# Gate and up by seven products: the first weight tile of a pair is split earlier, and its differences move on GpSimd

## The chip, the cores and the metric

The kernel runs on one core of a Trainium2 chip. Five engines work beside each other, each through its own instructions in program order: TensorE (PE, matmuls), VectorE (DVE), ScalarE (ACT), GpSimd (POOL) and SyncE (SP), whose queue issues the DMAs. The time is the device time of one execution in microseconds, the median of several runs. Lower is better.

## The reference

The program computes four transformer layers over 512 tokens of width 1024 in float32: two hybrid layers (retention, dilated attention, spatial gating) and two of a second kind (sparse attention or convolution, then cross attention). Each ends in the same feed-forward block, which is all that the change touches:

```python
def swiglu(xn, w_gate, w_up, w_down):
    return (jax.nn.silu(xn @ w_gate) * (xn @ w_up)) @ w_down
```

The hidden width is 2816, 22 column blocks of 128.

## The kernel before

**Float32 from three products.** Each operand is split into a high half (rounded to fp32r) and a low half (the rest), and `mm3` (lines 384 to 387) adds up high x high, high x low and low x high. For a weight tile of 128 x 1024 the high half is a cast on ScalarE and the low half a subtraction on VectorE. Line 249 and 250 do this for plain tiles in `pump`, line 266 and 270 for the tiles of a pair.

**Gate and up.** `ffn` (line 565) runs four times, once a layer. Column blocks 0 and 1 are computed plainly at the start, beside the end of the work before. Blocks 2 to 21 go two by two, once for gate and once for up, by seven products in the place of eight (Strassen's scheme in Winograd's form): 10 block pairs, two each, so 20 **units** a stage. A unit takes a pair of weight tiles: a first tile `a` with the blocks b11 and b21, a second tile `b` with b12 and b22. `W.unit()` (line 257) prepares them in place by named steps:

- `cast1`, `low1`: the first tile's high half (ScalarE L266) and low half (VectorE L270)
- `t13`: two differences of 128 x 512 on GpSimd (L283 and L284), which overwrite the first tile's b11 and the second tile's b12, and so come after cast1 and low1
- `cast4`, `low4`: the halves of b22 as it was (512 wide)
- `t24`: two more differences on VectorE (L287 and L288), which read what L283 wrote
- `cast2`, `low2`: the halves of the second tile, which is now t3 and t2
- `cast3`, `low3`: the halves of the first tile, which is now t1 and t4

`seven(i)` (line 668) issues the seven products of unit i, 12 matmuls of 128 x 256 each: a11 and a12 with slot s1, then s4, twice s2, twice s3. Behind each product a step `s0` to `s6` reads PSUM and prepares the units that follow: m1 is copied on ScalarE (L700), VectorE adds (L705, L714, L718, L723, L724), and at `s0` of the next unit `whole_sum` (L684), for a gate unit with a Silu on ScalarE (L686), or, for an up unit, a product of gate and up (L690).

**What sets the order.** The program order of the code is each engine's order; nothing is reordered by a planner here. Before the change, during unit i, cast1 of unit i+2 stands at s6, low1 of unit i+1 at s0, t13 at s1, t24 and cast2 at s4, low2 and cast3 at s5, low3 at s6. So low1 and the two GpSimd differences come in the first quarter of a unit and are wanted by t24 in its middle. Weight tiles come by DMA on SP's queue, the first tiles into three buffers, the second into two; a buffer is freed at low3 and low2. A split takes one of eight `hl` slots in turn.

**PSUM.** The third product lies in bank 2 in even units and in bank 7 in odd ones (line 672).

**Around the stage.** At its start `transposer` (line 399) turns the normalized input; behind its casts (L395) copies of the last two token blocks (L417) go to a buffer from which the sums of the scheme are made (`whole`, L629, two of them on GpSimd; `mix`, L633). During the last unit `W.pump(1)` after each product begins to split the down product's weight tiles, and `hsplit` (line 744) splits the hidden blocks: block 0 after the sixth product, block 1 behind the stage. The down product (line 788) then takes all eight banks, two for each of four token blocks.

Of the kernel before, what the change touches and what calls it, by code (L numbers as in the profile page):

```python
# [199 lines left out]
class _Weights:  # L200
# [53 lines left out]
            if not moved:  # L254
                return

    def unit(self):

        V, S, G = self.nc.vector, self.nc.scalar, self.nc.gpsimd
        u = {}  # L260

        def cast(name, src, n=D):
            def go():
                if name not in u:
                    u[name] = self.slot()
                S.copy(u[name][:, 0, :n], src())  # L266
            return go

        def low(name, src, n=D):
            return lambda: V.tensor_sub(u[name][:, 1, :n], src(), u[name][:, 0, :n].bitcast(F32))  # L270

        def fetch():
            while self.widths[self.split] > 0:
                self.pump(1, True)
            self.prefetch()
            u["a"], u["j"] = self.r.pop(self.split), self.split + 1
            self.split += 2
            u["b11"], u["b21"] = (u["a"][:, 512 * i:512 * i + 512] for i in range(2))

        def t13():  # L280
            b = u["b"] = self.r.pop(u["j"])
            u["b12"], u["b22"] = (b[:, 512 * i:512 * i + 512] for i in range(2))
            G.tensor_sub(u["b11"], u["b12"], u["b11"])  # L283
            G.tensor_sub(u["b12"], u["b12"], u["b22"])  # L284

        def t24():
            V.tensor_sub(u["b22"], u["b22"], u["b11"])  # L287
            V.tensor_sub(u["b21"], u["b21"], u["b22"])  # L288

        def free(i):  # L290
            def go():
                self.held[i] -= 1
                self.prefetch()
            return go
        one, two, last = (lambda: u["a"]), (lambda: u["b"]), (lambda: u["b22"])
        u["do"] = {
            "cast1": (fetch, cast("s1", one)), "low1": (low("s1", one),), "t13": (t13,), "t24": (t24,),
            "cast2": (cast("s2", two),), "low2": (low("s2", two), free(1)), "cast4": (cast("s4", last, 512),),
            "low4": (low("s4", last, 512),), "cast3": (cast("s3", one),), "low3": (low("s3", one), free(0)),
        }  # L300
        for k, slot, i in (("b11", "s1", 0), ("b21", "s1", 1), ("t3", "s2", 0), ("t2", "s2", 1), ("b22", "s4", 0),
                           ("t1", "s3", 0), ("t4", "s3", 1)):
            u["w" + k] = lambda slot=slot, i=i: [
                u[slot][:, z, 512 * i:512 * i + 512].rearrange("p (a c) -> p a c", c=P) for z in range(2)]
        return u
# [17 lines left out]
def tile_mixers(ctx: ExitStack, tc: tile.TileContext, a: dict, widths: list, out: bass.AP):  # L323
# [48 lines left out]
    def bank(i):  # L372
        return psum.tile([P, T], F32, tag=f"b{i}", name=f"b{i}")
# [25 lines left out]
    def transposer(xn, t, dst, banks):  # L399
        dh, dl = dst  # L400

        def go(halves=(0, 1)):
            for half in halves:
                b = bank(banks[half])
                for kk in range(4):
                    k = 4 * half + kk
                    PE.transpose(b[:, kk * P:(kk + 1) * P], xn[:, k * P:(k + 1) * P], ident)  # L407
                ks = slice(4 * half, 4 * half + 4)
                if dl is None:
                    S.copy(dh[:, ks, cols(t)], blocks(b))  # L410
                else:
                    split_from(dh[:, ks, cols(t)], dl[:, ks, cols(t)], blocks(b))
                    if keep["x"] is not None and dh is xh and t > 1:
                        kept.append((keep["x"][half][:, :, (t - 2) * P:(t - 1) * P], blocks(b)))
                        keep["t"].add(t)
            while kept:
                S.copy(*kept.pop(0))  # L417
        return go

    turned = {}  # L420
# [144 lines left out]
    def ffn(pend, post, nxt, last=False):  # L565
# [82 lines left out]

        def unit(i):
            if i not in ops:  # L650
                ops[i] = W.unit()
            return ops[i]

        def prep(i, *names):
            if 0 <= i < len(units):
                for name in names:
                    for f in unit(i)["do"][name]:
                        f()
# [9 lines left out]
        def seven(i):  # L668


            n, j = units[i]
            b1, b2, b3, b6, b7, b45 = (bank(k) for k in (0, 1, 2 + 5 * (i % 2), 3, 4, 5 + i % 2))
            p1, p2, p3, p6, p7 = (z[:, :256] for z in (b1, b2, b3, b6, b7))
            p4, p5 = b45[:, :256], b45[:, 256:]
            m1, u2, u3, u4 = (st["pc"][:, 256 * k:256 * k + 256] for k in range(4))
            if not j:
                c = hraw[:, n:n + 2, :]
            elif n + 2 < NF:
                c = hraw[:, n + 2:n + 4, :]
            else:  # L680
                c = base.tile([P, D], F32, tag="xn", name="up", bufs=2).rearrange("p (a c) -> p a c", a=2)

            def whole_sum():
                V.tensor_add(c[:, :, 256:], u3[:, None, :].to_broadcast([P, 2, 256]), halves(b45))  # L684
                if not j:
                    S.activation(c, c, AF.Silu)  # L686

            def gated():
                if j:
                    V.tensor_mul(hraw[:, n:n + 2, :], hraw[:, n:n + 2, :], c)  # L690
            done.append((whole_sum, gated))
            last = done[-2] if i else (lambda: None,) * 2

            def s0():
                last[0]()
                W.done(int(i > 0))
                prep(i + 1, "low1")

            def s1():
                S.copy(m1, p1)  # L700
                prep(i + 1, "t13")
                last[1]()

            def s2():
                V.tensor_add(c[:, 0, TOK[0]], m1, p2)  # L705
                prep(i + 1, "cast4")
                W.done()

            def s3():
                prep(i + 1, "low4")  # L710
                W.done()

            def s4():
                V.tensor_add(u2, m1, p6)  # L714
                prep(i + 1, "t24", "cast2")

            def s5():
                V.tensor_add(u3, u2, p7)  # L718
                prep(i + 1, "low2", "cast3")
                W.done()  # L720

            def s6():
                V.tensor_add(u4, u2, p5)  # L723
                V.tensor_add(c[:, 1, TOK[0]], u4, p3)  # L724
                prep(i + 1, "low3")
                prep(i + 2, "cast1")
            todo = (("a11", "b11", p1), ("a12", "b21", p2), ("s4", "b22", p3), ("s2", "t2", p6), ("s3", "t3", p7), ("s1", "t1", p5),
                    ("a22", "t4", p4))
            for r, (p, f) in enumerate(zip(todo, (s0, s1, s2, s3, s4, s5, s6))):
                product(i, *p)  # L730
                f()
                if i == 0 and r == 0:
                    sum_low("s1", 3)()
                if i == len(units) - 1:
                    if r == 5:
                        hsplit(0)
                    W.pump(1)
                W.prefetch()
                yield

# [3 lines left out]
        def hsplit(k):  # L744
            if k < NF and k not in hsp:
                t = shared()
                split_from(t[:, 0:T], t[:, T:2 * T], hraw[:, k, :])
                hsp[k] = (t[:, 0:T], t[:, T:2 * T])

        def also(i, *fs):  # L750
            us, g = steps[i]
            steps[i] = (us, lambda: (g(), [f() for f in fs]))
        late = len(steps) - 4
        keep.update(x=(quarter(full(0)), quarter(full(3))), t=set())

        def fill(t):
            if t not in keep["t"] and turned[t]:
                for half in range(2):
                    z = [y[:, 4 * half:4 * half + 4, cols(t)].bitcast(F32) for y in (xh, xl)]
                    G.tensor_add(keep["x"][half][:, :, (t - 2) * P:(t - 1) * P], *z)  # L760
                keep["t"].add(t)

        def unit0(*names):
            return lambda: prep(0, *names)
        also(0, whole(1, 0, 0, G), unit0("cast1"))
        also(1, whole(2, 4, 0, G), unit0("low1"))
        also(2, lambda: fill(2))
        also(late - 1, lambda: fill(2), lambda: fill(3), lambda: keep.update(x=None), unit0("t13", "cast4"), mix(3, 0, 3, 1), mix(4, 3, 1, 0), mix(2, 2, 4, 0),
             sum_high("s2", 4), sum_high("s4", 2))
        also(late, unit0("low4"), sum_low("s4", 2), unit0("t24", "cast2"), sum_low("s2", 4))  # L770
        also(late + 1, unit0("low2"), mix(0, 0, 1, 0), sum_high("s3", 0))
# [8 lines left out]
            g = seven(i)  # L780
            steps += [(12 * 0.119, lambda g=g: next(g))] * 7
        steps.append((0, last_sums))
        steps.append((0, lambda: (two(0), nxt(), hsplit(1))))

        TAIL = 4
        acc = {}
# [1197 lines left out]
```

## Time and profile before

| what | us |
|---|---|
| median of 3 runs (2798.55 to 2804.01) | 2798.68 |
| the profiled execution | 2799.59 |
| its span, first to last instruction | 2797.8 |
| TensorE busy | 2677.8 (96%) |
| VectorE busy | 1809.4 (65%) |
| ScalarE busy | 1182.2 (42%) |
| GpSimd busy | 782.4 (28%) |

The profile covers one execution. A row of the timeline gives start, duration, engine, line, operation, out<-in, size and count; in brackets the idle time before it and what ended it. `raw` is a weight tile as loaded, `hl` its split, `sh` a split activation or hidden block, `xh` and `xl` the split input, `pc` the buffer of m1, u2, u3 and u4, `hraw` the hidden values, `b` a PSUM bank. Busy TensorE includes the time in which matmuls overlap, so its share says little of how close to its pace it is. The four stages start at about 281, 894, 1700 and 2448 us.

### The profile page before, as it was taken

The numbers are of one execution on the slowest core, as the hardware profiler recorded it, in microseconds if no ns is written. First come the engines' busy times: TensorE is split into PE (matmuls) and PEld (weight loads), VectorE is DVE, ScalarE is ACT, GpSimd is POOL, SyncE is SP. The second block draws the span as 40 slices with busy tenths as digits, with TensorE's granted clock in tenths as the row PEclk, the third lists the DMA queues.
The fourth block names the chain that finished last, engine by engine and source line by source line (L and its number), as shares of the span: only waits on it lengthen the run. The fifth ranks groups of instructions, "written<-read, shape, count | busy, mean of one in ns | idle before, by whom it ended". The sixth has DMA issues, their size and how long they took to land.

```text
span 2797.8 us, 41468 instructions
## 1 busy us (share of the span) xinstructions
PE 2677.8 (96%) x16568; PEld 2378.7 (85%) x16568; DVE 1809.4 (65%) x2733; ACT 1182.2 (42%) x2015; POOL 782.4 (28%) x662
## 2 busy tenths in 40 slices
PE   8999999999999999999999999999998889999999
PEld 7888999889788999878677889998886578899987
DVE  4555888545565888453985437887379744488852
ACT  3434444333434444333444434444256544344431
POOL 3231333002232232012451312331049913133300
PEclk9999999999999999999999999999999999999999
DMA  4221232323121323423232212333232312133331
GB/s 154 78 68 67 91 106 98 130 75 108 61 80 53 102 98 101 138 70 102 64 124 83 91 38 91 106 103 124 91 119 91 113 30 92 46 91 106 99 116 65
DMA packets 76225, 256.42 MB, mean 92 GB/s; under 512 B 10368, under 2 KB 11776, under 8 KB 76032
## 3 DMA queue, kind: packets, MB, share of 16 engines
q1 hardware_dynamic: 76032, 253.77, 28.3%
q8 instruction: 130, 2.13, 0.3%
q14 instruction: 63, 0.52, 0.1%
HBM read 251.64 MB, written 2.10 MB: 91 GB/s over the span
## 4 chain that ended last, share of the span: by engine, by line
PE 51%; DVE 23%; POOL 12%; ACT 10%; issue 4%; DMA 1%; POOLq 0%; ACTq 0%; DVEq 0%; SPq 0%
PE b L385 15%; PE b L387 15%; PE b L386 14%; DVE hl L270 8%; ACT hl L266 5%; POOL raw L283 5%; POOL raw L284 4%; DVE raw L287 2%; DVE hl L250 2%; DVE b L1759 2%; DVE hraw L684 2%; ACT hl L249 1%; PE b L407 1%; PE b L1639 1%; DVE xn L430 1%
## 5 line engine op out<-in xcount | busy, mean ns | idle before, releaser
L385 PE MATMUL b<-xh,hl 128*128 128x256 f32 (+1 forms) x1728 | 505.5, 293 | 4.0 <-DVE xn L457 2.4
L386 PE MATMUL b<-xl,hl 128*128 128x256 f32 (+1 forms) x1728 | 504.1, 292 | 1.7 <-DVE xl L396 1.7
L387 PE MATMUL b<-xh,hl 128*128 128x256 f32 (+1 forms) x1728 | 503.6, 291 | 0.0
L266 ACT CAST hl<-raw 128x1024 fp32r<-128x1024 f32 x320 | 286.7, 941 | 391.1 <-DVE raw L287 391.1
L385 PE MATMUL b<-hl,xh 128*128 128x512 f32 (+2 forms) x1152 | 439.1, 381 | 4.9 <-ACT xh L395 3.1
L386 PE MATMUL b<-hl,xh 128*128 128x512 f32 (+2 forms) x1152 | 422.6, 367 | 1.7 <-DVE hl L250 1.7
L387 PE MATMUL b<-hl,xl 128*128 128x512 f32 (+2 forms) x1152 | 423.0, 367 | 0.2
L270 DVE TENSOR_TENSOR hl<-raw,hl 128x1024 fp32r<-128x1024 f32 x320 | 387.1, 1210 | 9.4 <-ACT hl L266 1.3
L250 DVE TENSOR_TENSOR hl<-raw,hl 128x1024 fp32r<-128x1024 f32 (+2 forms) x249 | 303.4, 1232 | 137.8 <-ACT hl L249 135.7
L249 ACT CAST hl<-raw 128x1024 fp32r<-128x1024 f32 (+2 forms) x308 | 303.5, 1000 | 101.9 <-PE b L387 60.1
L385 PEld LDWEIGHTS b<-xh,hl 128*128 128x128 f32 x1728 | 331.4, 192 | 11.4 <-issue 3.4
L386 PEld LDWEIGHTS b<-xl,hl 128*128 128x128 f32 x1728 | 331.3, 192 | 7.8 <-DVE xl L396 2.7
L387 PEld LDWEIGHTS b<-xh,hl 128*128 128x128 f32 x1728 | 331.2, 192 | 5.4
L283 POOL TENSOR_TENSOR raw<-raw 128x512 f32<-128x512 f32 x80 | 140.2, 1752 | 567.3 <-DVE hl L270 502.7
L387 PE MATMUL b<-hl,sh 128*128 128x512 f32 x704 | 276.3, 392 | 7.2 <-DVE sh L396 7.2
L385 PE MATMUL b<-hl,sh 128*128 128x512 f32 x704 | 276.7, 393 | 2.2 <-ACT sh L395 2.2
L387 PE MATMUL b<-sh,hl 128*128 128x256 f32 x960 | 270.8, 282 | 5.8 <-DVE hl L270 5.8
L386 PE MATMUL b<-hl,sh 128*128 128x512 f32 x704 | 276.0, 392 | 0.0
L385 PE MATMUL b<-sh,hl 128*128 128x256 f32 x960 | 269.2, 280 | 1.1 <-ACT hraw L576 1.1
L386 PE MATMUL b<-sh,hl 128*128 128x256 f32 x960 | 267.9, 279 | 0.0
L385 PEld LDWEIGHTS b<-hl,xh 128*128 128x128 f32 x1152 | 219.3, 190 | 35.1 <-issue 7.0
L386 PEld LDWEIGHTS b<-hl,xh 128*128 128x128 f32 x1152 | 219.4, 190 | 25.9 <-DVE hl L250 3.0
(304 smaller groups left out, 4745.2 us busy)
## 6 DMA issues: line engine op xcount, KB each, us to landing
raw<-in_ws SPq DMA_DIRECT2D x400, 512.0 KB, 3.6
raw<-in_ws SPq DMA_DIRECT2D x64, 384.0 KB, 3.1
x<-in_x SPq DMA_DIRECT2D x4, 512.0 KB, 6.6
mem<-in_mem SPq DMA_DIRECT2D x4, 512.0 KB, 5.6
out<-x SPq DMA_DIRECT2D x4, 512.0 KB, 2.6
raw<-in_ws SPq DMA_DIRECT2D x4, 336.0 KB, 2.8
gain<-in_g_mix_pre SPq DMA_DIRECT2D x2, 512.0 KB, 4.7
gain<-in_g_mix_post SPq DMA_DIRECT2D x2, 512.0 KB, 4.4
```

Of the source, the lines that this page charges most:

```text
L249: self.nc.scalar.copy(t[:, 0, :w], r[:, :w])
L250: self.low.tensor_sub(t[:, 1, :w], r[:, :w], t[:, 0, :w].bitcast(F32))
L266: S.copy(u[name][:, 0, :n], src())
L270: return lambda: V.tensor_sub(u[name][:, 1, :n], src(), u[name][:, 0, :n].bitcast(F32))
L283: G.tensor_sub(u["b11"], u["b12"], u["b11"])
L284: G.tensor_sub(u["b12"], u["b12"], u["b22"])
L287: V.tensor_sub(u["b22"], u["b22"], u["b11"])
L385: PE.matmul(o, lh, rh, start=first, stop=False)
L386: PE.matmul(o, lh, rl, start=False, stop=False)
L387: PE.matmul(o, ll, rh, start=False, stop=last)
L684: V.tensor_add(c[:, :, 256:], u3[:, None, :].to_broadcast([P, 2, 256]), halves(b45))
L1759: V.scalar_tensor_tensor(acc[g], i, w, acc[g], op0=OP.mult, op1=OP.add)
```

## The change

The first tile of a pair is split nearly a unit earlier: during unit i, cast1 of unit i+2 goes to s4 and low1 of unit i+2 to s5, and its t13 follows on GpSimd at s6. Unit 1 is prepared as before, and unit 0's t13 is done on VectorE. In the last unit the down tiles are pumped after every other product, and hidden blocks 0 and 1 are split after the fifth and sixth product. The banks of the third product swap between even and odd units. At the stage's start the copies of the turned input come at a later place (`flush`), and the two sums `whole` go from GpSimd to VectorE.

```diff
         def t13():
...
-            G.tensor_sub(u["b11"], u["b12"], u["b11"])
-            G.tensor_sub(u["b12"], u["b12"], u["b22"])
+            e = V if first else G
+            e.tensor_sub(u["b11"], u["b12"], u["b11"])
+            e.tensor_sub(u["b12"], u["b12"], u["b22"])
...
-            while kept:
-                S.copy(*kept.pop(0))
...
-                ops[i] = W.unit()
+                ops[i] = W.unit(not i)
...
-            b1, b2, b3, b6, b7, b45 = (bank(k) for k in (0, 1, 2 + 5 * (i % 2), 3, 4, 5 + i % 2))
+            b1, b2, b3, b6, b7, b45 = (bank(k) for k in (0, 1, 7 - 5 * (i % 2), 3, 4, 5 + i % 2))
...
             def s0():
                 last[0]()
                 W.done(int(i > 0))
-                prep(i + 1, "low1")
+                if not i:
+                    prep(1, "low1")
 
             def s1():
                 S.copy(m1, p1)
-                prep(i + 1, "t13")
+                if not i:
+                    prep(1, "t13")
                 last[1]()
...
             def s4():
                 V.tensor_add(u2, m1, p6)
                 prep(i + 1, "t24", "cast2")
+                prep(i + 2, "cast1")
 
             def s5():
                 V.tensor_add(u3, u2, p7)
+                prep(i + 2, "low1")
                 prep(i + 1, "low2", "cast3")
                 W.done()
 
             def s6():
                 V.tensor_add(u4, u2, p5)
                 V.tensor_add(c[:, 1, TOK[0]], u4, p3)
+                prep(i + 2, "t13")
                 prep(i + 1, "low3")
-                prep(i + 2, "cast1")
...
                 if i == len(units) - 1:
-                    if r == 5:
-                        hsplit(0)
-                    W.pump(1)
+                    if r in (0, 2, 4, 6):
+                        W.pump(1)
+                    if r in (4, 5):
+                        hsplit(r - 4)
...
-        also(0, whole(1, 0, 0, G), unit0("cast1"))
-        also(1, whole(2, 4, 0, G), unit0("low1"))
-        also(2, lambda: fill(2))
+        us, g = steps[0]
+        steps[0] = (us, lambda g=g: (whole(1, 0, 0, V)(), g()))
+        also(0, whole(2, 4, 0, V), unit0("cast1"))
+        also(1, unit0("low1"))
+        also(2, flush, lambda: fill(2))
...
-        steps.append((0, lambda: (two(0), nxt(), hsplit(1))))
+        steps.append((0, lambda: (two(0), nxt())))
```

In the changed file the lines of this part stand one up or down: L283 and L284 become L284 and L285, L287 becomes L288, L705 L706, L714 L715, L718 L720, L723 L726, L724 L727, L684 L683, L690 L689. L266 and L270 stay.

VectorE's row in the middle of a stage, over one unit, before; `raw_2847` is the second tile and `raw_2748` the first tile of the unit that is being prepared, `raw_2866` the first tile of the one after it:

```order
L287 TENSOR_TENSOR raw_2847<-raw_2847,raw_2748 128x512
L288 TENSOR_TENSOR raw_2748<-raw_2748,raw_2847 128x512
L718 TENSOR_TENSOR pc_2628<-pc_2628,b4_2992 128x256
L270 TENSOR_TENSOR hl_3067<-raw_2847,hl_3067 128x1024
L723 TENSOR_TENSOR pc_2628<-pc_2628,b6_2993 128x256
L724 TENSOR_TENSOR hraw_2336<-pc_2628,b7_2990 128x256
L270 TENSOR_TENSOR hl_3085<-raw_2748,hl_3085 128x1024
L684 TENSOR_TENSOR hraw_2336<-pc_2628,b6_2993 128x2x256
L270 TENSOR_TENSOR hl_3104<-raw_2866,hl_3104 128x1024
L690 TENSOR_TENSOR hraw_2336<-hraw_2336 128x1024
L705 TENSOR_TENSOR hraw_2336<-pc_2628,b1_3107 128x256
```

The same row after; `raw_2850`, `raw_2753` and `raw_2871` are the second tile, the first tile and the next unit's first tile:

```order
L288 TENSOR_TENSOR raw_2850<-raw_2850,raw_2753 128x512
L289 TENSOR_TENSOR raw_2753<-raw_2753,raw_2850 128x512
L720 TENSOR_TENSOR pc_2628<-pc_2628,b4_2995 128x256
L270 TENSOR_TENSOR hl_3069<-raw_2871,hl_3069 128x1024
L270 TENSOR_TENSOR hl_3067<-raw_2850,hl_3067 128x1024
L726 TENSOR_TENSOR pc_2628<-pc_2628,b6_2996 128x256
L727 TENSOR_TENSOR hraw_2336<-pc_2628,b2_2993 128x256
L270 TENSOR_TENSOR hl_3088<-raw_2753,hl_3088 128x1024
L683 TENSOR_TENSOR hraw_2336<-pc_2628,b6_2996 128x2x256
L689 TENSOR_TENSOR hraw_2336<-hraw_2336 128x1024
L706 TENSOR_TENSOR hraw_2336<-pc_2628,b1_3110 128x256
```

The next unit's low1 has moved from behind L684 to ahead of low2; nothing stands between L683 and L689 (or L706) now.

ScalarE's row over one unit before, from the 512-wide cast4 of a unit to the next unit's copy of m1; `raw_2569` is the second tile, `raw_2496` the first, `raw_2631` the next unit's first tile:

```order
L266 CAST hl_2801<-raw_2569 128x512
L266 CAST hl_2831<-raw_2569 128x1024
L266 CAST hl_2849<-raw_2496 128x1024
L266 CAST hl_2868<-raw_2631 128x1024
L700 COPY pc_2628<-b0_2870 128x256
```

After, where `raw_2494` is the first tile of that unit:

```order
L266 CAST hl_2801<-raw_2569 128x512
L266 CAST hl_2831<-raw_2569 128x1024
L266 CAST hl_2833<-raw_2631 128x1024
L266 CAST hl_2852<-raw_2494 128x1024
L700 COPY pc_2628<-b0_2873 128x256
```

cast1 of the next unit has gone from third to second of the three wide casts, behind cast2 and ahead of cast3.

VectorE at the end of a stage before, from the last `whole_sum` of a gate unit; `up` is the last up block, `hl_4891` and `hl_4909` are low halves of down tiles, `sh_4965` that of hidden block 0:

```order
L684 TENSOR_TENSOR hraw_2336<-pc_2628,b5_4761 128x2x256
L250 TENSOR_TENSOR hl_4891<-raw_4636,hl_4891 128x1024
L250 TENSOR_TENSOR hl_4909<-raw_4752,hl_4909 128x1024
L705 TENSOR_TENSOR up_4876<-pc_2628,b1_4871 128x256
L714 TENSOR_TENSOR pc_2628<-pc_2628,b3_4873 128x256
L718 TENSOR_TENSOR pc_2628<-pc_2628,b4_4874 128x256
L396 TENSOR_TENSOR sh_4965<-hraw_2336,sh_4965 128x512
L723 TENSOR_TENSOR pc_2628<-pc_2628,b6_4875 128x256
L724 TENSOR_TENSOR up_4876<-pc_2628,b7_4872 128x256
```

After; `sh_4952` is hidden block 0, `sh_4968` block 1:

```order
L683 TENSOR_TENSOR hraw_2336<-pc_2628,b5_4764 128x2x256
L250 TENSOR_TENSOR hl_4891<-raw_4641,hl_4891 128x1024
L706 TENSOR_TENSOR up_4876<-pc_2628,b1_4871 128x256
L250 TENSOR_TENSOR hl_4922<-raw_4757,hl_4922 128x1024
L715 TENSOR_TENSOR pc_2628<-pc_2628,b3_4873 128x256
L397 TENSOR_TENSOR sh_4952<-hraw_2336,sh_4952 128x512
L720 TENSOR_TENSOR pc_2628<-pc_2628,b4_4874 128x256
L397 TENSOR_TENSOR sh_4968<-hraw_2336,sh_4968 128x512
L726 TENSOR_TENSOR pc_2628<-pc_2628,b6_4875 128x256
L727 TENSOR_TENSOR up_4876<-pc_2628,b2_4872 128x256
```

Hidden block 0 comes ahead of L718, block 1 right behind it, and L724 reads bank 2 instead of bank 7.

More of the change, by code (lines that the diff above doesn't have):

```diff
@@ L255, in pump, with unit @@
                 return
-    def unit(self):
+    def unit(self, first=False):
         V, S, G = self.nc.vector, self.nc.scalar, self.nc.gpsimd
@@ L754, in ffn, with flush @@
         keep.update(x=(quarter(full(0)), quarter(full(3))), t=set())
+        def flush():
+            while kept:
+                S.copy(*kept.pop(0))
         def fill(t):
@@ L764, in unit0 @@
             return lambda: prep(0, *names)
-        also(0, whole(1, 0, 0, G), unit0("cast1"))
-        also(1, whole(2, 4, 0, G), unit0("low1"))
-        also(2, lambda: fill(2))
-        also(late - 1, lambda: fill(2), lambda: fill(3), lambda: keep.update(x=None), unit0("t13", "cast4"), mix(3, 0, 3, 1), mix(4, 3, 1, 0), mix(2, 2, 4, 0),
+        us, g = steps[0]
[3 more added lines that the diff above has]
+        also(2, flush, lambda: fill(2))
+        also(late - 1, flush, lambda: fill(2), lambda: fill(3), lambda: keep.update(x=None), unit0("t13", "cast4"), mix(3, 0, 3, 1), mix(4, 3, 1, 0), mix(2, 2, 4, 0),
              sum_high("s2", 4), sum_high("s4", 2))
```

## The prediction

> **What bounds the kernel now.** I read the page's head first, then the list of waits, then the gate-and-up stage on each engine in order of time.
>
> ```profile
> span 2797.8 us, 41468 instructions
> ...
> PE b L387 <- DVE hl L270: 5.8, 24, 0.3
> PE b L387 <- DVE sh L396: 7.2, 4, 1.8
> ACT hl L266 <- DVE raw L287: 391.1, 80, 7.0
> ```
>
> In the waits the columns are microseconds in all, times, longest. TensorE waits for a low half (L270) 24 times, six in each of the four gate-and-up stages, and four times, once a stage, for L396, the first low half of the down product. Both are VectorE's work, so the question is VectorE's pace. Its rows from one L287 (a unit's differences) to the next are:
>
> ```profile
> 308.20 0.69 DVE L287 TENSOR_TENSOR raw<-raw 128x512 f32<-128x512 f32 x1 [0.86 <-POOL raw L284]
> ...
> 451.76 0.69 DVE L287 TENSOR_TENSOR raw<-raw 128x512 f32<-128x512 f32 x1 [0.85 <-POOL raw L284]
> 452.49 0.69 DVE L288 TENSOR_TENSOR raw<-raw 128x512 f32<-128x512 f32 x1
> 453.10 0.41 DVE L718 TENSOR_TENSOR pc<-pc,b 128x256 f32<-128x256 f32 x1
> 453.57 1.23 DVE L270 TENSOR_TENSOR hl<-raw,hl 128x1024 fp32r<-128x1024 f32 x1
> 454.71 0.41 DVE L723 TENSOR_TENSOR pc<-pc,b 128x256 f32<-128x256 f32 x1
> 455.16 0.42 DVE L724 TENSOR_TENSOR hraw<-pc,b 128x256 f32<-128x256 f32 x1
> 455.50 1.22 DVE L270 TENSOR_TENSOR hl<-raw,hl 128x1024 fp32r<-128x1024 f32 x1
> 456.63 0.68 DVE L684 TENSOR_TENSOR hraw<-pc,b 128x512 f32<-128x512 f32 x1
> ...
> 458.70 0.42 DVE L705 TENSOR_TENSOR hraw<-pc,b 128x256 f32<-128x256 f32 x1 [0.25 <-ACT pc L700]
> 459.22 1.15 DVE L270 TENSOR_TENSOR hl<-raw,hl 128x512 fp32r<-128x512 f32 x1
> ...
> 461.56 0.69 DVE L287 TENSOR_TENSOR raw<-raw 128x512 f32<-128x512 f32 x1 [0.85 <-POOL raw L284]
> ...
> 492.78 0.69 DVE L287 TENSOR_TENSOR raw<-raw 128x512 f32<-128x512 f32 x1 [0.86 <-POOL raw L284]
> ```
>
> From 308.20 (second unit of the stage) to 492.78 (the last) lie 18 units: 184.58 us, 10.25 a unit, 20.51 a pair. TensorE on its own is a little quicker:
>
> ```profile
> 381.25 0.28 PE L385 MATMUL b<-sh,hl 128*128 128x256 f32 x1
> ...
> 391.25 0.28 PE L385 MATMUL b<-sh,hl 128*128 128x256 f32 x1
> ...
> 392.79 0.28 PE L386 MATMUL b<-sh,hl 128*128 128x256 f32 x1
> 393.33 0.39 PE L387 MATMUL b<-sh,hl 128*128 128x256 f32 x1 [0.27 <-DVE hl L270]
> ```
>
> A unit without a stall takes it 10.00 (381.25 to 391.25), a pair 20.0. It uses up its slack over nine units and is then stopped once a pair (0.54 instead of 0.12 between the last two rows). **VectorE's in-order loop, with its waits, sets the stage**; TensorE's 96% hides that. So I price that loop.
>
> **The loop after the change.** What goes: VectorE's 0.85 in front of L287, since GpSimd's two differences now end most of a unit earlier, and GpSimd's hold on L270 128x512 (1.15 to 1.23 there, 0.69 for a 512-wide L287). What comes: in VectorE's row the low half of the first tile of the unit after next ("low1") moves from behind L684 to ahead of the second tile's low half ("low2"). Its cast ("cast1") moves on ScalarE to just behind the second tile's cast ("cast2"), which needs L287. ScalarE's rows:
>
> ```profile
> 452.49 2.94 ACT L266 CAST hl<-raw 128x1024 fp32r<-128x1024 f32 x3 [6.97 <-DVE raw L287]
> ...
> 457.35 1.06 ACT L686 ACTIVATE hraw<-hraw 128x1024 f32<-128x1024 f32 x1 [1.91 <-DVE hraw L684]
> ```
>
> Three casts in 2.94 at 1.05 each start 0.945 apart. The first ends 0.03 before the L270 at 453.57; the second would let low1 start at 454.51, 1.41 after L718 (453.10), where before 0.47 passed. So **a new ScalarE wait of 0.94 a unit** takes the place of GpSimd's 0.85. Behind it on VectorE stand low2, L723, L724 and everything that TensorE asks for.
>
> The second price is hidden in the old order. After L684, every other unit has a Silu (L686) and then a copy (L700), which L705 needs: 456.63 to 458.70 is 2.07. Before, low1 (1.14) ran inside that time; now nothing does.
>
> Third, who holds up whom beside GpSimd:
>
> ```profile
> 447.82 2.21 POOL L283 TENSOR_TENSOR raw<-raw 128x512 f32<-128x512 f32 x1 [6.80 <-DVE hl L270]
> ...
> 447.66 1.22 DVE L690 TENSOR_TENSOR hraw<-hraw 128x1024 f32<-128x1024 f32 x1
> 449.01 0.42 DVE L705 TENSOR_TENSOR hraw<-pc,b 128x256 f32<-128x256 f32 x1
> 449.35 1.23 DVE L270 TENSOR_TENSOR hl<-raw,hl 128x512 fp32r<-128x512 f32 x1
> ```
>
> L283, issued during L690 (ends 448.88), ends 1.15 after it, at 450.03; the L270 begun at 449.35 ends only 0.55 after that, a loss of 0.54; L705, which reads a PSUM bank, isn't touched. In the new order L283 starts beside low2 (start T), ends at T+1.22+1.15 = T+2.37 and holds the third low half ("low3", at T+1.93) for 0.44, less 0.14 as above: 0.30. L284 then waits for low3, ends at T+4.60 and holds L690 (at T+4.08), in the units that have it, for 0.38.
>
> The sum, start to start, for a unit with Silu: 0.73 (L287 to L288), 0.61 (to L718), 1.41 (to low1), 1.14 (low1, as 453.57 to 454.71), 1.14 (low2), 0.45, 0.34, 1.13+0.30 (low3), 2.07 (L684 to L705), 0.52 (to the 512-wide L270), 0.61 (as L288), 0.34 (L714, as L705 to L270 at 449.35) = 10.79. With L690 in place of Silu the first eight are the same 7.25, then 0.72 (L690 reads what L684 wrote: 0.68 and 0.04), 1.14+0.38, 0.34, 0.61, 0.34: 10.78. **A pair takes 21.57 instead of 20.51**, and TensorE's 20.0 can't hide that. Nine pairs a stage, four stages: 36 x 1.06 = **+38.2 us**. Bounds: without any hold by GpSimd a pair is 20.59 (+2.9 in all); if each hold is as long as the 0.54 measured, and the free 512-wide L270 is held too, 21.57 + 0.24 + 0.24 + 0.16 + 2 x 0.54 = 23.29 would be the far end (+100). I take 21.57, which is the measured pattern moved; for the range I take 22.21 (+61), since the 512-wide L270 comes after L284 has ended.
>
> **The rest.** The end of a stage:
>
> ```profile
> 497.66 0.68 DVE L684 TENSOR_TENSOR hraw<-pc,b 128x512 f32<-128x512 f32 x1
> 500.40 2.44 DVE L250 TENSOR_TENSOR hl<-raw,hl 128x1024 fp32r<-128x1024 f32 x2 [2.06 <-ACT hl L249]
> ...
> 503.95 0.68 DVE L396 TENSOR_TENSOR sh<-hraw,sh 128x512 fp32r<-128x512 f32 x1
> ...
> 505.00 0.42 DVE L724 TENSOR_TENSOR up<-pc,b 128x256 f32<-128x256 f32 x1
> ...
> 501.33 0.28 PE L387 MATMUL b<-xh,hl 128*128 128x256 f32 x1
> ...
> 504.69 0.50 PE L387 MATMUL b<-hl,sh 128*128 128x512 f32 x1 [1.80 <-DVE sh L396]
> ```
>
> The down product starts in earnest when L396 ends (504.63). In the new row it is L250, L705, L250, L714, L396: 500.40 + 1.14 + 0.34 + 1.14 + 0.34 + 0.69 = 504.05, 0.58 earlier; four stages, -2.3. But the third product of the last unit now lies in bank 2, not 7. The down product's second token block needs bank 2 after four more matmuls; L724, its last reader, now ends 1.74 after L396 (0.61 + 0.34 + 0.61 + 0.45 + 0.42, less L396's own 0.69). At 0.20 a matmul (17 in 3.42, below) TensorE is there after 0.86: a new wait of 0.88, +3.5 in all.
>
> The granted clock stands behind this stop:
>
> ```profile
> 501.89:505.30 3.41, 1.35 (x5) 0.82 (x6) 3.27 (x7) 3.15 (x6) 0.00 (x0) 1.00 0.71 217
> 505.30:508.71 3.41, 3.41 (x10) 2.63 (x9) 3.38 (x6) 2.37 (x4) 0.00 (x0) 0.50 0.72 258
> 508.71:512.13 3.42, 3.42 (x17) 2.79 (x16) 3.42 (x4) 0.35 (x1) 0.00 (x0) 1.00 0.84 277
> ...
> 1925.24:1928.66 3.42, 3.42 (x10) 2.65 (x9) 3.39 (x5) 1.94 (x4) 0.00 (x0) 0.50 0.57 192
> ...
> 2672.76:2676.18 3.42, 3.42 (x9) 2.64 (x8) 3.37 (x6) 2.33 (x3) 0.00 (x0) 0.50 0.31 125
> ```
>
> (Busy time and count of PE, PEld, VectorE, ScalarE, GpSimd; then the clock.) A stretch with TensorE busy 1.35 of 3.41 is followed by one at clock 0.50, in three of the four stages: 10 matmuls instead of 17, 7 x 0.20 = 1.4 lost. After the change low2 of the last unit has no low1 ahead of it, TensorE isn't stopped there and stops 1.3 before L396's end instead of 3.2; with two matmuls in between and 0.88 later it idles some 1.8 in two pieces. I take the drop as gone: -4.2, other end 0. The Trainium skill, "TensorE: Matmul & The Clock Gate", section "What's actually happening", has the low clock come only after a whole idle window of about 3.4 us; the rows above, with 1.35 busy, don't agree, and by the page the -4.2 would fall away.
>
> The start of a stage:
>
> ```profile
> 273.92 2.98 DVE L250 TENSOR_TENSOR hl<-raw,hl 128x1024 fp32r<-128x1024 f32 x1 [1.60 <-ACT hl L249]
> ...
> 281.72 2.31 DVE L430 SCALAR_TENSOR_TENSOR xn<-x,sm,gain 128x1024 f32<-128x1024 f32 x1 [0.77 <-POOL sm L392]
> ```
>
> Both run beside GpSimd; freed, L250 falls to 1.22, and L430 may lose as much as a hold of 1.0. VectorE gets two sums (1.14 each, one of them inside the 1.60 of waiting) and two differences (0.73 + 0.61): between -2 and +1 a stage. I take -1 in all. The copies behind the casts (L417) leave ScalarE's casts earlier; that is in this term.
>
> Sum: 38.2 - 2.3 + 3.5 - 4.2 - 1 = +34 on the profiled execution of 2799.59 (its span 2797.8 and 1.8 around it); the median, 2798.68, is 0.9 lower. Forecast: **2833 us**.
>
> **The rivals.** *The holds don't come, and nothing changes.* Without GpSimd's holds a pair is 20.59: +2.9 - 2.3 + 3.5 - 4.2 - 1 = -1, 2798. Against it: L283 beside L690 shows the hold. *Faster.* The new ScalarE wait is the one place that decides. If cast1 were done before L287 releases cast2, 0.94 a unit goes and a pair is 21.57 - 1.88 = 19.7, under TensorE's 20.0; from 20.0 down the stage is TensorE's. Then the 24 stops (0.42 each, 10) and of the end 2.3 + 4.2 go, with the start's 1 and bank 2's 3.5 back: 2785. Against it: ScalarE waits 80 times for L287 with a cast at the head of its row. The Trainium skill, "TensorE: Matmul & The Clock Gate", section "Architectural detail: the array is 16x 32x32, not 1x 128x128", calls ScalarE's queue strictly in order; by that this rival needs VectorE to run ahead of TensorE, and the list of waits speaks against it. *The change doesn't do what it says:* second tiles land so late that GpSimd ends late all the same. Then 0.85 a unit comes back on top, 72 x 0.85 = 61: 2894. A second tile's buffer is freed a unit earlier, 10 us, so I give this little.
>
> **How the numbers follow.** Forecast 0.73 (2812 to 2857, by the hold and clock terms), no change 0.11, faster 0.12, late tiles 0.04. A measurement can tell about 0.2%, 5.6 us, from no change. Faster 0.12, same 0.11, slower 0.77. The range takes in the case without holds: 2797 to 2857.
>
> **What would show it.** L270 of low1 waiting for ScalarE's L266 in each unit, about 1 us; L287 to L287 21.5 a pair; no idle time ahead of L287 for GpSimd; TensorE stopped about 0.8 in almost every unit, some 17 times a stage, from the second or third unit on; clock 0.50 gone behind the stages. I am wrong if L287 comes at 20.0 a pair with TensorE's stops gone, or if L684 to L705 isn't 2.07 without low1 between.

## The result and the profile after

| | us |
|---|---|
| after, median of 4 runs (2839.23 to 2846.06) | 2841.28 |
| before, median of 4 runs beside them (2798.55 to 2804.01) | 2800.61 |
| ratio, 95% interval | 1.0146 (1.0129 to 1.0164) |
| span of the profiled execution, before and after | 2797.8, 2837.3 |

The changed kernel is 1.5% slower; 2833 was forecast, with 2797 to 2857 as the range. The list of waits of the changed kernel (microseconds in all, times, longest) shows what has come in the place of GpSimd:

```profile
span 2837.3 us, 41388 instructions
...
ACT hl L266 <- DVE raw L288: 350.3, 80, 7.6
...
DVE hl L270 <- ACT hl L266: 73.8, 76, 1.0
...
DVE hraw L706 <- ACT pc L700: 49.9, 36, 1.4
...
PE b L388 <- DVE hl L270: 43.9, 72, 1.1
```

VectorE waits 76 times for a cast of ScalarE ahead of a low half: in each stage once 0.33 at its start, as before, and 18 times about 1.01, once in each unit from 1 to 18. 36 times, once a pair, it waits 1.4 for the copy L700 that stands behind the Silu. TensorE is stopped 72 times for a low half, 18 times a stage; before it was 24 times and 5.8 us in all, now it is 43.9. The wait for GpSimd ahead of the differences (65.1, 76 times, before) has shrunk to 3.4 us in four, one a stage, for unit 1, which is prepared as before.

VectorE's row over a pair, in order of time (start, duration, engine, line, operation, out<-in):

```profile
440.31 1.52 DVE L270 TENSOR_TENSOR hl<-raw,hl 128x1024 fp32r<-128x1024 f32 x1
441.75 0.68 DVE L683 TENSOR_TENSOR hraw<-pc,b 128x512 f32<-128x512 f32 x1
443.81 0.42 DVE L706 TENSOR_TENSOR hraw<-pc,b 128x256 f32<-128x256 f32 x1 [1.38 <-ACT pc L700]
...
445.27 0.69 DVE L288 TENSOR_TENSOR raw<-raw 128x512 f32<-128x512 f32 x1
...
446.60 0.41 DVE L720 TENSOR_TENSOR pc<-pc,b 128x256 f32<-128x256 f32 x1
448.02 2.36 DVE L270 TENSOR_TENSOR hl<-raw,hl 128x1024 fp32r<-128x1024 f32 x2 [1.01 <-ACT hl L266]
...
451.08 1.52 DVE L270 TENSOR_TENSOR hl<-raw,hl 128x1024 fp32r<-128x1024 f32 x1
452.53 0.67 DVE L683 TENSOR_TENSOR hraw<-pc,b 128x512 f32<-128x512 f32 x1
453.24 1.61 DVE L689 TENSOR_TENSOR hraw<-hraw 128x1024 f32<-128x1024 f32 x1
454.98 0.42 DVE L706 TENSOR_TENSOR hraw<-pc,b 128x256 f32<-128x256 f32 x1
...
456.25 0.69 DVE L288 TENSOR_TENSOR raw<-raw 128x512 f32<-128x512 f32 x1
...
499.77 0.69 DVE L288 TENSOR_TENSOR raw<-raw 128x512 f32<-128x512 f32 x1
```

The new wait for cast1 stands ahead of the two low halves at 448.02 (1.01), the bare Silu chain between L683 and L706 (441.75 to 443.81, 2.06), and the two holds by GpSimd are the 1.52 and 1.61 in the place of 1.22. From L288 to L288 the unit at 445.27 takes 10.98; the unit ahead of it, whose sums have the Silu, took 10.79. A stage's 18 units take 195.83 (303.93 to 499.77), where it was 184.58.

ScalarE and GpSimd beside this:

```profile
442.46 1.06 ACT L685 ACTIVATE hraw<-hraw 128x1024 f32<-128x1024 f32 x1 [4.30 <-DVE hraw L683]
443.42 0.35 ACT L700 COPY pc<-b 128x256 f32<-128x256 f32 x1
443.68 0.62 ACT L266 CAST hl<-raw 128x512 fp32r<-128x512 f32 x1
445.99 2.95 ACT L266 CAST hl<-raw 128x1024 fp32r<-128x1024 f32 x3 [1.69 <-DVE raw L288]
```

```profile
449.33 2.20 POOL L284 TENSOR_TENSOR raw<-raw 128x512 f32<-128x512 f32 x1 [6.35 <-DVE hl L270]
451.60 2.17 POOL L285 TENSOR_TENSOR raw<-raw 128x512 f32<-128x512 f32 x1
```

The three wide casts form one block that begins when L288 has ended; the middle one is cast1, whose tile has nothing to do with L288. L284 covers the start of low3, L285 that of L689. TensorE at its stops in two units:

```profile
449.64 0.28 PE L387 MATMUL b<-sh,hl 128*128 128x256 f32 x1
450.44 0.39 PE L388 MATMUL b<-sh,hl 128*128 128x256 f32 x1 [0.52 <-DVE hl L270]
...
460.42 0.28 PE L387 MATMUL b<-sh,hl 128*128 128x256 f32 x1
461.42 0.39 PE L388 MATMUL b<-sh,hl 128*128 128x256 f32 x1 [0.72 <-DVE hl L270]
```

Matmuls that are 0.12 apart otherwise are 0.80 and 1.00 apart here, in every unit from 1 to 18: TensorE now goes at VectorE's pace.

### The profile page after: what moved, and what is told of

Read it like the earlier page. It is cut to its first block, busy times and chain, and to the rows that moved or that the text cites. A ratio compares the mean times of both kernels' runs of the same rounds, so it can differ in the third digit from the quotient of the medians.

```text
span 2837.3 us, 41388 instructions
## 1 busy us (share of the span) xinstructions
PE 2684.9 (95%) x16568; PEld 2376.9 (84%) x16568; DVE 1808.7 (64%) x2749; ACT 1181.4 (42%) x2015; POOL 820.4 (29%) x646
## 4 chain that ended last, share of the span: by engine, by line
PE 61%; DVE 22%; ACT 7%; issue 6%; POOL 3%; DMA 1%; DVEq 0%; ACTq 0%; POOLq 0%; SPq 0%
PE b L388 18%; PE b L386 18%; PE b L387 18%; DVE hl L270 9%; ACT hl L266 4%; DVE hraw L689 2%; DVE hl L250 2%; DVE b L1769 1%; PE b L408 1%; ACT hl L249 1%; PE b L1649 1%; DVE raw L288 1%; PE b L1802 1%; DVE xn L429 1%; DVE hraw L683 1%
## 5 line engine op out<-in xcount | busy, mean ns | idle before, releaser
L266 ACT CAST hl<-raw 128x1024 fp32r<-128x1024 f32 x320 | 287.2, 942 | 350.3 <-DVE raw L288 350.3
L270 DVE TENSOR_TENSOR hl<-raw,hl 128x1024 fp32r<-128x1024 f32 x320 | 367.2, 1166 | 77.6 <-ACT hl L266 73.8
L250 DVE TENSOR_TENSOR hl<-raw,hl 128x1024 fp32r<-128x1024 f32 (+2 forms) x249 | 298.2, 1211 | 132.3 <-ACT hl L249 130.2
L284 POOL TENSOR_TENSOR raw<-raw 128x512 f32<-128x512 f32 x76 | 167.2, 2200 | 549.7 <-DVE hl L270 549.7
L388 PE MATMUL b<-sh,hl 128*128 128x256 f32 x960 | 276.1, 288 | 43.9 <-DVE hl L270 43.9
```

Of the source, the lines that this page charges most:

```text
L250: self.low.tensor_sub(t[:, 1, :w], r[:, :w], t[:, 0, :w].bitcast(F32))
L284: e.tensor_sub(u["b11"], u["b12"], u["b11"])
L388: PE.matmul(o, ll, rh, start=False, stop=last)
```

## The experiments

The times of single executions of one kernel differ by several microseconds (before, beside the first four experiments: 2794.49 to 2804.42 in 13 runs), and the mean granted clock goes with them: 0.990 in the shortest of the 13, 0.987 in the longest. So where a kernel was timed once, the loop from L288 to L288 is what is compared; it repeats within 0.03 in all units but one or two.

**e1: cast1 ahead of cast2.** One line is moved, no work is changed.

```diff
             def s4():
                 V.tensor_add(u2, m1, p6)
+                prep(i + 2, "cast1")
                 prep(i + 1, "t24", "cast2")
-                prep(i + 2, "cast1")
```

> Only the order of two casts on ScalarE changes: cast1 of the unit after next stands ahead of cast2, not behind it. Theory (VectorE waits for cast1 behind cast2, 0.94 a unit): a pair of units on VectorE falls from 21.77 by 1.88 to 19.9, under TensorE's 20.0, so the 18 units take about 180 instead of 196 in each stage: 2778 us, faster than the kernel before. Rival (GpSimd's holds on the shared inputs are what lengthened the loop): 2835 or more, a pair at 21.5 or more.

Measured: 2773.30 (2765.18 to 2773.97, 4 runs) against 2803.34 before, ratio 0.9889 (0.9873 to 0.9905). VectorE, the list of waits, and TensorE of this kernel:

```profile
442.82 0.69 DVE L288 TENSOR_TENSOR raw<-raw 128x512 f32<-128x512 f32 x1
...
444.15 0.41 DVE L720 TENSOR_TENSOR pc<-pc,b 128x256 f32<-128x256 f32 x1
444.48 2.35 DVE L270 TENSOR_TENSOR hl<-raw,hl 128x1024 fp32r<-128x1024 f32 x2
...
452.51 0.68 DVE L288 TENSOR_TENSOR raw<-raw 128x512 f32<-128x512 f32 x1
...
459.39 1.61 DVE L689 TENSOR_TENSOR hraw<-hraw 128x1024 f32<-128x1024 f32 x1
...
462.40 0.68 DVE L288 TENSOR_TENSOR raw<-raw 128x512 f32<-128x512 f32 x1
```

```profile
DVE hl L270 <- ACT hl L266: 1.3, 4, 0.3
```

```profile
478.69 0.28 PE L386 MATMUL b<-sh,hl 128*128 128x256 f32 x1
...
488.69 0.28 PE L386 MATMUL b<-sh,hl 128*128 128x256 f32 x1
```

low1 follows L720 0.33 later instead of 1.42; GpSimd's hold on L689 is as it was (1.61). A pair takes 9.69 + 9.89 = 19.58, 2.18 less than after: the whole wait (1.42 - 0.33 = 1.09), twice. No stop of TensorE for L270 is left on the list; a unit takes it 10.00, so TensorE sets the pace now. The wait for ScalarE's cast is enough to account for the slowdown, since taking it away alone makes this kernel faster than both others. It is not the only one of which that holds, as e9 will show.

**e2: the three moved steps back, the rest of the change kept.**

```diff
             def s0():
-                if not i:
-                    prep(1, "low1")
+                prep(i + 1, "low1")
             def s1():
-                if not i:
-                    prep(1, "t13")
+                prep(i + 1, "t13")
             def s4():
-                prep(i + 2, "cast1")
             def s5():
-                prep(i + 2, "low1")
             def s6():
-                prep(i + 2, "t13")
                 prep(i + 1, "low3")
+                prep(i + 2, "cast1")
```

> The changed kernel with cast1, low1 and t13 of units 1 to 19 back at their old steps; the start, the last pair and the banks stay changed. Theory: the loop is 20.5 a pair again, 45 us go: 2796, some 5 under the kernel before. Rival (the start, the end or the banks cost what was lost): 2830 or more.

Measured: 2799.79 (2794.39 to 2803.22, 10 runs), ratio 0.9991 (0.9980 to 1.0003): no change that can be told. The loop is that of before to a hundredth, 9.79 and 10.71, 184.55 for 18 units, with GpSimd ahead of the differences again:

```profile
439.74 0.69 DVE L288 TENSOR_TENSOR raw<-raw 128x512 f32<-128x512 f32 x1 [0.85 <-POOL raw L285]
```

So everything that the loop lost lies in the moved steps; all the rest of the change is worth, beside the old loop, something between -6 and +1 us.

**e3: cast1 early, low1 and the differences where they were.** The edit is that of e2, but cast1 stays at s4 behind cast2.

> The changed kernel with low1 and t13 back at their old steps and cast1 alone still early, behind cast2. Theory (cast1's place costs only because low1 waits for it ahead of low2): 20.5 a pair, 2796. Rival (cast1 ahead of cast3 makes cast3 and low3 late, and that is the loss): 21.5 or more a pair, 2835.

Measured: 2806.50 in one run; the loop takes 9.85 and 10.71, 20.56 a pair, 0.05 more than before. The place of the cast costs nothing as long as no VectorE instruction ahead of TensorE's need waits for it. The time was expected 10 us lower. The 0.05 a pair is 1.8 of that, and a window at half clock that I had taken as gone still stands behind the first stage (at 505), some 1.6; the rest is not explained, and single runs differ by as much. The loop, not the time, decides here.

**e4: without GpSimd's differences.**

```diff
             def s6():
...
-                prep(i + 2, "t13")
+                if i + 2 < len(units):
+                    u = unit(i + 2)
+                    u["b"] = W.r.pop(u["j"])
+                    u["b12"], u["b22"] = (u["b"][:, 512 * k:512 * k + 512] for k in range(2))
```

> The changed kernel without the two GpSimd differences of units 2 to 19 (they are left out, so gate and up are computed from other blocks). Theory (holds of 0.30 in each unit and 0.38 in every second): a pair at 21.77 - 0.98 = 20.8, 2806. Rival (the holds cost nothing, ScalarE's waits are all): 21.77, 2841.

Measured: 2806.18 in one run. VectorE, in the unit with the product:

```profile
444.60 1.22 DVE L270 TENSOR_TENSOR hl<-raw,hl 128x1024 fp32r<-128x1024 f32 x1
445.74 0.68 DVE L683 TENSOR_TENSOR hraw<-pc,b 128x512 f32<-128x512 f32 x1
446.45 1.22 DVE L689 TENSOR_TENSOR hraw<-hraw 128x1024 f32<-128x1024 f32 x1
447.81 0.42 DVE L706 TENSOR_TENSOR hraw<-pc,b 128x256 f32<-128x256 f32 x1
```

low3 and L689 are back at 1.22. A pair takes 10.47 + 10.29 = 20.76, so GpSimd's holds cost 0.32 in a unit with Silu and 0.68 in the other, as priced (0.30 and 0.68). That is 1.00 a pair, beside 2.18 for the cast's wait (e1), and without them the loop is still slower than before's 20.51. L706 follows L689 by 1.36 here, with no hold at all.

**e5: the Silu one step later.** It is issued at s1, behind the copy m1.

```diff
             def whole_sum():
                 V.tensor_add(c[:, :, 256:], u3[:, None, :].to_broadcast([P, 2, 256]), halves(b45))
-                if not j:
-                    S.activation(c, c, AF.Silu)
 
             def gated():
                 if j:
                     V.tensor_mul(hraw[:, n:n + 2, :], hraw[:, n:n + 2, :], c)
+                else:
+                    S.activation(c, c, AF.Silu)
```

> The changed kernel with the Silu of a gate unit issued behind the next unit's copy of m1 instead of ahead of it. Theory (L706 waits for Silu and copy in every second unit, and low1 no longer fills that time): L683 to L706 falls from 2.07 to 0.6, the 512-wide L270 behind it is held 0.16 by L285, a pair falls from 21.77 by 1.5 to 20.3 and the kernel to 2787. Rival (that wait overlaps with the one for cast1, so only one of them counts): 21.5 or more a pair, 2835.

Measured: 2826.42 in one run, 39 us above what I expected. A pair takes 10.51 + 10.97 = 21.48, 0.28 less and not 1.5. That is the rival's number, but the wait for cast1 isn't the reason. VectorE and ScalarE show why:

```profile
441.78 0.68 DVE L683 TENSOR_TENSOR hraw<-pc,b 128x512 f32<-128x512 f32 x1
442.38 0.41 DVE L706 TENSOR_TENSOR hraw<-pc,b 128x256 f32<-128x256 f32 x1
444.09 0.69 DVE L270 TENSOR_TENSOR hl<-raw,hl 128x512 fp32r<-128x512 f32 x1 [1.31 <-ACT hl L266]
```

```profile
442.49 1.06 ACT L689 ACTIVATE hraw<-hraw 128x1024 f32<-128x1024 f32 x1 [4.04 <-DVE hraw L683]
443.45 0.60 ACT L266 CAST hl<-raw 128x512 fp32r<-128x512 f32 x1
```

L706 doesn't wait any more, but the next instruction, the 512-wide low4, does: its cast4 now stands behind the Silu. I had moved the wait by one instruction, 1.38 at L706 to 1.31 at low4.

**e9: the Silu behind cast4.** A third function `silu` in `done`, called at s2; the sums are as in e5.

```diff
+            def silu():
+                if not j:
+                    S.activation(c, c, AF.Silu)
-            done.append((whole_sum, gated))
+            done.append((whole_sum, gated, silu))
...
                 prep(i + 1, "cast4")
+                last[2]()
```

> After, with the Silu issued one step later still, behind cast4, the next unit's fourth cast (in e5 it stood ahead of cast4, and the fourth subtraction then waited 1.31 us for that cast). Theory (the Silu is 1.06 us of ScalarE in a place where VectorE waits for whatever stands behind it; put behind the last cast, VectorE waits for it nowhere): the step from the unit's high-half sum to the next unit's difference loses both waits, L288 to L288 of a Silu unit goes from 10.79 to about 9.2 and a pair from 21.77 to about 20.2, so 18 units take about 181.5 and not 195.9; a time near 2785. First rival (the Silu delays cast2 and cast1 of the next unit instead, as it delayed cast4): the wait comes back ahead of the first or second subtraction, a pair stays at 21.4 and the time near 2826, as in e5. Second rival (the prediction's price of 2.07 a pair was wrong, because the wait of cast1 behind cast2 takes back what the Silu gives): the pair falls by less than 0.6, a time of 2820 to 2830.

Measured: 2785.61 (2778.68 to 2788.10, 4 runs) against 2799.83, ratio 0.9941 (0.9924 to 0.9957).

```profile
447.32 0.69 DVE L288 TENSOR_TENSOR raw<-raw 128x512 f32<-128x512 f32 x1
...
454.58 0.68 DVE L683 TENSOR_TENSOR hraw<-pc,b 128x512 f32<-128x512 f32 x1
455.18 0.41 DVE L708 TENSOR_TENSOR hraw<-pc,b 128x256 f32<-128x256 f32 x1
455.51 0.85 DVE L270 TENSOR_TENSOR hl<-raw,hl 128x512 fp32r<-128x512 f32 x1
...
456.62 0.68 DVE L288 TENSOR_TENSOR raw<-raw 128x512 f32<-128x512 f32 x1
...
467.60 0.69 DVE L288 TENSOR_TENSOR raw<-raw 128x512 f32<-128x512 f32 x1
```

The unit with L683 at 454.58 takes 9.30 (447.32 to 456.62), the next 10.98: 20.28 a pair, 1.49 less than after, though the wait for cast1 stays. So the missing cover of the Silu's chain costs 1.49 a pair, and e5 missed because of the cast behind the Silu. It also shows that either of the two waits, taken away, brings the loop below before's 20.51.

**e6: e1 and e5 together.**

> cast1 ahead of cast2 and the Silu behind the copy, both. Theory: VectorE's loop is under TensorE's 20.0 a pair with the first alone (19.6 measured), so the second adds nothing that TensorE can use: 2770 to 2776, like cast1 first alone. Rival (VectorE still sets the stage there): a further 1.5 a pair, 2720 to 2740.

Measured: 2775.63 (2769.82 to 2777.08, 4 runs), ratio 0.9911 (0.9892 to 0.9930), not told apart from e1. VectorE's units take 9.42 and 9.90 until it has caught up with TensorE, then 10.01: once TensorE is the bound, a shorter VectorE loop gives nothing.

**e7: before, with the Silu as in e5.**

> The kernel before with the same move of the Silu. Theory (there low1 fills the time, and L287 waits for GpSimd's second difference, which follows low1): L287 to L287 stays 9.8 and 10.7, 2798 to 2804. Rival (the Silu cost time before too): 0.3 a pair less, 2788.

Measured: 2792.01 in one run, with the loop of before to the hundredth (9.80 and 10.71, 184.54). Before, the Silu's chain cost nothing: low1 covered most of it, as the prediction had it, and the 0.25 that was left at L705 stood ahead of a wait of 0.85 for GpSimd. The rival's 0.3 a pair isn't there. The lower time comes with windows at half clock in other places, none behind a stage.

**e8: after, with the old banks.**

```diff
-            b1, b2, b3, b6, b7, b45 = (bank(k) for k in (0, 1, 7 - 5 * (i % 2), 3, 4, 5 + i % 2))
+            b1, b2, b3, b6, b7, b45 = (bank(k) for k in (0, 1, 2 + 5 * (i % 2), 3, 4, 5 + i % 2))
```

> The changed kernel with the third product's banks as before. Theory: only the 0.8 wait for bank 2 at the second token block of the down product goes (1.72 from the first waiting matmul to that block becomes about 1.0), and TensorE waits 0.4 at the first unit's third product again, which costs nothing since VectorE is behind there: 2838. Rival (the banks matter inside the units): a pair other than 21.77.

Measured: 2841.02 in one run. TensorE at the start of the first down product, after, then with the old banks:

```profile
511.06 0.50 PE L388 MATMUL b<-hl,sh 128*128 128x512 f32 x1 [0.90 <-DVE sh L397]
...
512.78 0.50 PE L386 MATMUL b<-hl,sh 128*128 128x512 f32 x1 [0.52 <-DVE up L727]
```

```profile
514.38 0.50 PE L388 MATMUL b<-hl,sh 128*128 128x512 f32 x1 [0.90 <-DVE sh L397]
...
515.42 0.39 PE L386 MATMUL b<-hl,sh 128*128 128x512 f32 x1
```

From the matmul that waits for the low half to the second token block it is 1.72 after and 1.04 with the old banks, with the wait for L727 gone. Over the 22 matmuls from the first of these on it is 5.92 to 5.96 after and 5.14 to 5.16 here: 0.80 a stage, some 3 us in all. In one run's total that can't be seen. A pair takes 10.79 + 10.98 = 21.77 as after, so the banks don't matter inside the units.

## Why the prediction was right, point by point

The sum of the profiled executions, 2837.3 - 2797.8 = 39.5:

| step | predicted | measured |
|---|---|---|
| the loop, 18 units in four stages | +38.2 | +45.5 |
| the wait at the stage's end | -2.3 | -2.5 |
| bank 2 | +3.5 | +3.3 |
| half clock behind three stages | -4.2 | -4.9 |
| the stage's start | -1 | -1.6 |
| sum | +34 | +39.8 |

The sum is near 39.5 in part by luck. Two stretches that no step covers differ between the two executions: what lies ahead of the first stage is 2.9 shorter after (L250 at 260.91 before and 257.98 after), and what lies between the second stage and the third is 2.5 longer. The windows at half clock lie in other places there (one at 212 before, none there after).

- **The wait for cast1.** Predicted 0.94 a unit, 1.41 from L718 to low1: 446.60 to 448.02, 1.42. e1 took it away alone, and its 2 x 1.09 a pair with it. The rival "faster" needed just that, cast1 done ahead of cast2; the change didn't give it, one line did. Its 2785 was still 12 too high: it took 2.3 off the stages' ends and put 3.5 on for bank 2, but in e1 TensorE isn't stopped at a stage's end at all, while the changed kernel is stopped there for 0.90 and 0.52. The Trainium skill's rule of queues strictly in order ("TensorE: Matmul & The Clock Gate", section "Architectural detail: the array is 16x 32x32, not 1x 128x128") agrees with these rows: cast1, which needs nothing of L288, waited behind cast2, which does.
- **The Silu chain without low1.** Predicted 2.07, measured 2.06; e7 shows that it cost nothing before, e9 that it costs 1.49 a pair after.
- **GpSimd's holds.** Predicted 0.30 and 0.38, measured by e4 as 0.32 a unit and 0.36 more beside the product. The Trainium skill, "SBUF — State Buffer", section "Who interferes with whom", says that a VectorE instruction with two inputs in SBUF contends with a GpSimd instruction that reads SBUF, and that one with at most one, outside the two-port modes, does not. The trace agrees: low3 and L689 (1.52 and 1.61 for 1.22) end late, while L683, which reads a PSUM bank, keeps its 0.67 at 452.53 beside L285. "No change" (no holds) falls with e4, and wouldn't have held either: without them a pair is 20.76, where I had 20.59.
- **The step that was mis-sized** is L690 to L705 in the sum of 10.78. I took 1.14 + 0.38, a 128x1024 instruction followed 0.08 before its end; the row quoted there had 447.66 to 449.01, 1.35. With that 1.35 the sum is 10.99, measured 10.98. The missing 7.3 us are this step (36 x 0.19 = 6.8, by the pairs of the first stage) and one unit of the second stage that took 0.35 longer. With 1.35 in the sum the forecast would have been 2841.
- **The stage's end.** L288 of the last unit to the first matmul that waits for L397 went from 11.91 to 11.29 (499.77 to 511.06), 0.62 earlier (0.58 predicted). Bank 2 was priced 0.88 a stage; the 22 matmuls from that one on take 5.92 to 5.96 in place of 5.12 (second stage of before, full clock), 0.82 on average, and 0.80 of it goes with the old banks (e8).
- **The half clock.** Those 22 matmuls took 6.74 to 6.76 before in the three stages with the drop, 1.63 more than at full clock. The 1.4 a stage of the prediction was 7 x 0.20; at full clock these matmuls start 0.23 apart (the 17 takes in some that only reach into the window), and 7 x 0.23 = 1.6. After, no window behind a stage is at 0.50:

```profile
510.31:513.73 3.42, 2.15 (x8) 1.48 (x9) 3.35 (x8) 2.33 (x3) 0.00 (x0) 1.00 0.75 256
513.73:517.14 3.41, 3.41 (x17) 2.80 (x16) 3.41 (x5) 2.10 (x3) 0.00 (x0) 1.00 0.82 279
```

  (Behind the length stand five busy times with counts, then the clock.) The number came, but the reason is shown only in part. Before, the second stage had the same stops as the others (0.56 and 1.80) and no drop. With the changed end beside the old loop the drop still stood behind two stages in e2 and behind one in e3; in the seven kernels with the moved steps (after, e1, e4, e5, e6, e8, e9) it stood behind none of 28. So it goes with the longer stop, but where the stop falls counts too. The busy time of a window doesn't decide it either: after, a window with 2.43 busy (from 1329.51) is followed by one at 0.51, and before, one with 1.63 (from 2280.20) by one at 1.00. The Trainium skill, "TensorE: Matmul & The Clock Gate", section "What's actually happening", asks for a whole idle window. The rows behind the stages of before measure otherwise, and they decide.
- **Stage starts.** Counted from the work just ahead, L288 of unit 1 came 1.33 earlier in the first two stages and 0.55 later in the others, -1.6 in all.
- **Late second tiles** (2894): nothing of it, L288 doesn't wait for GpSimd beyond unit 1.

Not settled: why L706 begins 0.13 after L689 ends and not 0.08 ahead of it, as it does behind L683 in e5. It does so in before, after and e4, with and without a hold. The kernel has a likely reason, which no run tests: in these units L706 writes into the block of `hraw` that L689 has just read, so it has to wait until L689 has ended, as L689 waits for L683 (453.24, 0.04 after its end). In e5's unit with the Silu, L706 and L683 write and read different parts. A semaphore instruction of up to 0.05 stands ahead of L706 in the trace.

## What to carry to other kernels

A step that is moved earlier on one engine brings its producers with it: look at what stands ahead of them in their own in-order row, since a cast that needs nothing waits as long as the one it is put behind, and one line of order was worth 68 us here (2841 and 2773). A gap that another instruction happened to fill gets its full price when that instruction leaves, and moving the cause by one place only passes the wait to the next consumer (e5), until it stands behind the last one (e9). Price such a loop from start to start with rows of the same neighbours, not from a duration and a usual overlap.

## What the runs showed of the hardware

The clock of 0.50 came behind a window of 3.41 us with TensorE busy 1.35, and not behind one of 3.42 with 2.15. There is no threshold of busy time in these traces: it also came behind one with 2.43 busy (1329.51, after) and not behind one with 1.63 (2280.20, before). GpSimd's difference of 128x512 took 2.20 beside a VectorE low half and held the next low half back by 0.30, in each unit alike; a VectorE instruction that reads a PSUM bank kept its 0.67 beside the second difference (2.17).
